# A start stage in hand-written order, and decode logits by one multiply-and-sum instruction of VectorE per 128 channels

## The chip, the cores and the metric

The kernel runs on one NeuronCore of a Trainium2 chip. The metric is the device time of one execution in microseconds (us), as the median of several runs. The engines are called PE (TensorE, matmuls), PEld (its weight load), DVE (VectorE), ACT (ScalarE), POOL (GpSimd) and SP (SyncE, which only issues transfers here).

## The reference

One inference step of a decoder layer with two parallel branches: stick-breaking attention and a gated short convolution. 512 prompt rows with 16 learned rows ahead of them, and 8 decode sequences of 4 rows with 512 cached positions each, in pages of 128.

```python
h = rmsnorm(x, g_pre)                                        # (560 rows, 2048)
q, k, v, ga, cb, cc, ch, gc, ma, mc = jnp.split(h @ w_in, split_offsets(), axis=-1)
a = stick_breaking(q, k, v, ...) * silu(ga)                  # 8 heads of 128 channels
c = cb * conv3_causal(cc * ch) * silu(gc)
m = sigmoid(ma + b_ga) * (a @ w_pa) + sigmoid(mc + b_gc) * (c @ w_pc)
y = x + rmsnorm(m @ w_out, g_post)

def stick_breaking(q, k, v, q_pos, k_pos, b_sb):
    z = einsum('bqhd,bkhd->bhqk', q, k) * HEAD_DIM ** -0.5 + b_sb
    mask = k_pos < q_pos
    log_keep = where(mask, log_sigmoid(-z), 0.0)
    after = cumsum(log_keep, axis=3, reverse=True) - log_keep
    attn = where(mask, exp(log_sigmoid(z) + after), 0.0)
    return einsum('bhqk,bkhd->bqhd', attn, v)
```

For the decode rows the keys and values of the past are read from the paged cache through `page_table`. All arrays are fp32.

## The kernel before

**Split products.** Each fp32 operand of a large product is held as a rounded part ("hi", fp32r) and the remainder ("lo"). A product is three matmuls: hi x hi, hi x lo, lo x hi. ACT makes the hi part of a weight block by a cast (`whi`, 128x1024, L236, L309 in the start), DVE the lo part by a subtraction (`wlo`, L237, L290 in the start). A weight block is 8 tiles of 128x128; PE does 24 matmuls with it for one range of tokens. Three hi and three lo blocks are buffered (`whl`), five raw ones (`wraw`), which SP's queue loads.

**The start.** The 560 token rows come in five blocks, 0 to 4 (`XT`; block 4 has the last 8 prompt rows, the 32 decode rows and 8 learned rows). `norm_stats` loads a block and takes its sum of squares on ACT (L195); `rstd_of` takes the root by a logarithm and an exponential on ACT (L129, L130) and five Newton instructions on DVE (L133 to L137). `norm_half` scales half of the channels on DVE (`hn`, L205), transposes them on PE in two groups of four into PSUM tiles (L213), and copies those into `h_hi` on ACT (L219) and `h_lo` on DVE (L224). The queries of four heads (`FIRST`) are projected meanwhile (L297), head by head: blocks 0 and 1 first with the hi weights alone, and when blocks 4, 2 and 3 are there the missing terms and the other tokens.

**The heads.** For four heads (`head_now`) k, v and q are projected and attention is done at once; for the other four (`head_later`) k and v are projected and kept. `natural` transposes k or v into row order through a PSUM tile into `nat` (one buffer), from which POOL's queue writes the outputs.

**The decode logits.** `decode_steps` is a generator; each step handles one page for half of the heads of one decode sequence: 4 heads, 4 rows, 128 cached positions on the partitions. DVE multiplies the page with the queries of two rows at a time (`pr`, 128x1024, L689, twice), and the sums over 128 channels are taken on ACT by eight or twelve copies that accumulate (`junk`, L695) and on DVE by a reduction of the rest (L698). 6 of 16 units of 4 pages (24 steps) run among the heads ("part"), 40 among the gate projections ("logits"). `dec_step` and `dec_group` say where: `dec_group` is called after each pair of column blocks of the gate and convolution projections, 32 times up to the last logits.

**The gates.** Each pair of 128-column blocks is done by `seven`, seven block products (L887) with sums of weight blocks (`s`) on DVE (L899, L902, L910, L915).

**What sets the order.** The program is written in one order, and a scheduler reorders it by its own costs, except instructions wrapped in `pin` (`tc.keep_in_program_order`), which keep their written order among one another on their engine. Every engine runs its queue in order.

## Time and profile before

| | us |
|---|---|
| median of 3 runs (lowest, highest) | 1638.24 (1635.78, 1639.5) |
| the profiled execution | 1638.43 |
| its span | 1636.8 |
| PE busy | 1596.0 (98%) |
| PEld busy | 1534.2 (94%) |
| DVE busy | 1259.1 (77%) |
| ACT busy | 969.5 (59%) |
| POOL busy | 232.2 (14%) |

The shares are means over stages. The start lasts to about 86 us of the span, the heads to 397, the gate and convolution projections to about 1163, the two branch products to about 1444, and the last product and normalization to the end. Matmuls are pipelined and their ends are modelled, so the count of matmuls in a stretch says more on PE than its busy time. A wait is put down to the engine that came last by the profile.

### The profile page before, as it was taken

To read this page: it belongs to the slowest core of one execution; us is meant where nothing else is said; L and a number is where in the kernel's file an instruction comes from. 1 tells how busy PE (TensorE), PEld (TensorE's weight loads), DVE (VectorE), ACT (ScalarE), POOL (GpSimd) and SP (SyncE) were. 2 spreads that over 40 slices of the span, in tenths; PEclk is the share of its full clock that TensorE was granted. 3 is DMA by queue.
4 is the path that set the end of the run, shared out by engine and by line. 5 is a ranking of instruction groups with operands and counts; after the bars stand their busy time and mean duration, and the time that the engine had idled before them with its cause. 6 is when DMAs were issued, how large, how long until landed. Compare 5 with 4: busy or idle time off the path is not lost.

```text
span 1636.8 us, 31603 instructions
## 1 busy us (share of the span) xinstructions
PE 1596.0 (98%) x12172; PEld 1534.2 (94%) x12172; DVE 1259.1 (77%) x1730; ACT 969.5 (59%) x2528; POOL 232.2 (14%) x418
## 2 busy tenths in 40 slices
PE   7999999999999999999999999999999999999997
PEld 6999999999999999999999999989877799999997
DVE  4537887797988988888988888876565567887776
ACT  6237887755775656565676667686544453355562
POOL 0033233322101000100011011002122110000000
PEclk7999999999999999999999999999999999999999
DMA  9254554545554444343555554446888545533345
GB/s 228 77 171 143 157 163 138 152 121 171 157 155 136 130 130 130 116 141 114 148 150 151 156 175 147 128 130 202 263 265 246 179 141 165 183 89 101 106 124 192
DMA packets 306813, 252.72 MB, mean 154 GB/s; under 512 B 11522, under 2 KB 276806, under 8 KB 305846
## 3 DMA queue, kind: packets, MB, share of 16 engines
q1 hardware_dynamic: 278165, 160.45, 34.3%
q0 software_dynamic: 28368, 89.98, 16.9%
q8 instruction: 95, 1.56, 0.4%
q14 instruction: 57, 0.46, 0.1%
q10 hardware_dynamic: 128, 0.27, 0.1%
HBM read 217.95 MB, written 32.71 MB: 153 GB/s over the span
## 4 chain that ended last, share of the span: by engine, by line
PE 75%; ACT 6%; DMA 5%; DVE 4%; issue 3%; POOL 0%; DVEq 0%; SPq 0%; POOLq 0%; ACTq 0%
PE mm L887 24%; PE mm L252 24%; PE o L887 20%; ACT junk L695 3%; PE tp L784 2%; ACT whi L236 2%; PE z L614 1%; DMA raw<-in_w_in 1%; PE o L624 1%; DVE pr L689 1%; DMA gt<-gate_scr 1%; DVE wlo L237 1%; PE z L545 1%; PE z L1319 1%; DMA kpage<-in_cache_k 1%
## 5 line engine op out<-in xcount | busy, mean ns | idle before, releaser
L236 ACT CAST whi<-raw 128x1024 fp32r<-128x1024 f32 x247 | 258.9, 1049 | 253.6 <-PE o L887 75.6
L237 DVE TENSOR_TENSOR wlo<-raw,whi 128x1024 fp32r<-128x1024 f32 x247 | 301.5, 1221 | 56.7 <-ACT whi L236 45.4
L887 PE MATMUL mm<-h_hi,whi 128*128 128x272 f32 (+1 forms) x1152 | 333.8, 290 | 2.8 <-ACT whi L236 2.8
L887 PE MATMUL mm<-h_lo,whi 128*128 128x272 f32 (+1 forms) x1152 | 332.4, 289 | 0.0
L887 PE MATMUL mm<-h_hi,wlo 128*128 128x272 f32 (+1 forms) x1152 | 331.6, 290 | 0.0
L887 PE MATMUL o<-t_hi,whi 128*128 128x272 f32 (+1 forms) x864 | 253.1, 293 | 8.7 <-ACT o L901 5.0
L887 PE MATMUL o<-t_hi,wlo 128*128 128x272 f32 (+1 forms) x864 | 250.8, 290 | 1.3 <-DVE wlo L237 1.3
L887 PE MATMUL o<-t_lo,whi 128*128 128x272 f32 (+1 forms) x864 | 250.6, 290 | 0.0
L237 DVE TENSOR_TENSOR wlo<-s,whi 128x1024 fp32r<-128x1024 f32 x126 | 154.2, 1224 | 100.5 <-ACT whi L236 100.2
L887 PEld LDWEIGHTS mm<-h_hi,whi 128*128 128x128 f32 x1152 | 217.7, 189 | 5.4 <-ACT whi L236 3.7
L887 PEld LDWEIGHTS mm<-h_hi,wlo 128*128 128x128 f32 x1152 | 216.6, 189 | 0.6 <-DVE dr L412 0.4
L887 PEld LDWEIGHTS mm<-h_lo,whi 128*128 128x128 f32 x1152 | 217.1, 188 | 0.1
L695 ACT ACTIVATE junk<-pr 128x128 f32<-128x128 f32 x592 | 182.6, 309 | 28.5 <-DVE pr L689 16.3
L236 ACT CAST whi<-s 128x1024 fp32r<-128x1024 f32 x126 | 131.5, 1044 | 96.9 <-PE o L887 30.8
L252 PE MATMUL mm<-h_hi,whi 128*128 128x280 f32 (+1 forms) x640 | 188.1, 294 | 0.0
L252 PE MATMUL mm<-h_hi,wlo 128*128 128x280 f32 (+1 forms) x640 | 188.0, 295 | 0.0
L252 PE MATMUL mm<-h_lo,whi 128*128 128x280 f32 (+1 forms) x640 | 187.6, 293 | 0.0
L887 PEld LDWEIGHTS o<-t_hi,whi 128*128 128x128 f32 x864 | 163.6, 189 | 15.5 <-ACT o L901 6.1
L887 PEld LDWEIGHTS o<-t_hi,wlo 128*128 128x128 f32 x864 | 163.8, 190 | 2.2 <-DVE wlo L237 2.2
L887 PEld LDWEIGHTS o<-t_lo,whi 128*128 128x128 f32 x864 | 164.4, 190 | 0.0
L689 DVE TENSOR_TENSOR pr<-kpage,qb 128x1024 f32<-128x1024 f32 x128 | 152.3, 1218 | 10.7 <-DMA qb<-q_scr 6.5
L252 PEld LDWEIGHTS mm<-h_hi,whi 128*128 128x128 f32 x640 | 121.4, 190 | 0.7
(392 smaller groups left out, 3402.3 us busy)
## 6 DMA issues: line engine op xcount, KB each, us to landing
raw<-in_w_in SPq DMA_DIRECT2D x192, 512.0 KB, 4.3
kpage<-in_cache_k POOLq DMA_DIRECT2D x64, 256.0 KB, 3.4
qb<-q_scr POOLq DMA_DIRECT2D x32, 512.0 KB, 5.7
vpage<-in_cache_v POOLq DMA_DIRECT2D x64, 256.0 KB, 6.1
raw<-in_w_out SPq DMA_DIRECT2D x32, 512.0 KB, 4.0
gate_scr<-g POOLq DMA_DIRECT2D x32, 272.0 KB, 3.5
gt<-gate_scr POOLq DMA_DIRECT2D x16, 544.0 KB, 4.2
raw<-in_w_pc SPq DMA_DIRECT2D x16, 512.0 KB, 5.9
```

Source lines behind the costliest of these rows:

```text
L236: act.copy(hi, x)
L237: dve.tensor_sub(lo, x, hi.bitcast(F32))
L252: pe.matmul(o, lhsT=w, rhs=r[:, t0:t1], start=(k == 0 and n == 0), stop=(k == nk - 1 and n == 2))
L545: pe.matmul(zt[:m, c0:c0 + n], lhsT=l[:, s0:s0 + m], rhs=r[:, ts:ts + n], start=(c0 == 0 and i == 0), stop=(i == 2), skip_group_check=True)
L614: pe.matmul(o, lhsT=l, rhs=x, start=False, stop=(i == len(ops) - 1), skip_group_check=True)
L624: pe.matmul(ot[:, ts - NMETA:ts - NMETA + n], lhsT=l[:m, st, :], rhs=x[:m, c0:c0 + n], start=False, stop=(g == GROUPS[-1] and i == 2), ski ...
L689: dve.tensor_mul(pr, kt.unsqueeze(1).broadcast_to([P, 2, 512]), qt))
L695: act.activation(junk, pr[:, t, h * P:(h + 1) * P], AF.Copy, accum_out=z_all[:, pg, b, 4 * hf + h, 2 * i + t:2 * i + t + 1])
L784: pe.matmul(po[32 * j:32 * (j + 1), :], lhsT=lhs, rhs=rhs, start=(pg == 0), stop=(pg == NPG), tile_position=(0, 32 * j), skip_group_check= ...
L887: pe.matmul(o, lhsT=l[:, k, :], rhs=r, start=(start and k == 0 and m == 0), stop=(stop and k == 7 and m == 2), skip_group_check=True)
L1319: pin(pe.matmul(o, lhsT=(m1, m2)[h][:, k + 8 * (q == 1), ts], rhs=two[h][q == 2][:, :, k, :], start=(n == 0), stop=(n == 47)))
```

## The change

Three parts, in words and then in the diff.

1. **The start** is written out by hand and pinned on every engine, SP's queue too. A block's load is a step of its own (`x_load`) apart from its statistics. The weights of the four early heads come in eight chunks, each with 256 input channels of all four heads (`q_load`), rather than in eight blocks of one head each; the raw bytes are the same. `q_chunk` does all three terms of a chunk for the 256 tokens of blocks 0 and 1, into four accumulators in two PSUM banks; the other 296 tokens follow for all chunks, head by head. Two of the four copies of the norm's weight move from DVE to ACT, the Newton steps of blocks 2 and 4 from DVE to POOL, and the transposes go round five PSUM tiles instead of four.
2. **The logits.** The two multiplies, the accumulating copies on ACT and the reduction on DVE become 16 DVE instructions a page, each of which multiplies 128 channels of a head with a row's query and sums them. In the built program each is two entries of DVE's queue: the instruction, and a read of its sum.
3. **Buffers and places.** `nat` has two buffers and `qn` four instead of one. Head 0's first decode step moves from behind its k to behind its attention; the first gate groups make 0, 2, 2, 2 steps instead of 2, 1, 2, 1, and the later ones 1, 2 by turns so that all 40 are done by group 32. Some POOL transfers near the two places are pinned.

```diff
-    def rstd_of(eng, out, ss, tmp, n, w=1, later=False):
+    def rstd_of(eng, out, ss, tmp, n, w=1, later=False, fix=lambda ins: ins):
...
-        act.activation(r, ss, AF.Ln, bias=eps_c[:n], scale=1.0 / D)
-        act.activation(r, r, AF.Exp, scale=-0.5)
+        fix(act.activation(r, ss, AF.Ln, bias=eps_c[:n], scale=1.0 / D))
+        fix(act.activation(r, r, AF.Exp, scale=-0.5))
...
-        with tc.high_priority():
-            act.activation(sq, xt, AF.Square, accum_out=ss)
-            newton = rstd_of(dve, rs, ss, tmp, n, later=True)
-        return (i, n, xt, rs), newton
+        pin(act.activation(sq, xt, AF.Square, accum_out=ss))
+        return (i, n, xt, rs), rstd_of(eng, rs, ss, tmp, n, later=True, fix=pin)
...
+    def q_load():
+        c = len(q_raw)
+        raw = wraw.tile([P, 8, P], F32, tag="raw", name="raw")
+        pin(nc.sync.dma_start(raw.rearrange("p (k h) c -> p k (h c)", k=2),
+                              win[2 * c * P:2 * (c + 1) * P, GATE_Q:GATE_Q + FIRST * P].rearrange(
+                                  "(k p) c -> p k c", p=P)))
+        q_raw.append(raw)
...
+    def q_product(o, h, k, n, start, stop):
+        t0, t1 = START[n]
+        hi, lo = (by_k(x[k // 2])[:, k % 2, h, :] for x in (q_hi, q_lo))
+        for m, (l, r) in enumerate(((hi, h_hi), (hi, h_lo), (lo, h_hi))):
+            pin(pe.matmul(o, lhsT=l, rhs=r[:, k, t0:t1], start=(start and m == 0), stop=(stop and m == 2),
+                          skip_group_check=True))
...
+    X[0], X[1] = x_load(0), x_load(1)
+    for _ in range(3):
+        q_load()
+    X[2] = x_load(2)
+    X[0], newton0 = norm_stats(X[0])
+    g_copy(0), g_copy(1)
+    g_copy(2), g_copy(3)
+    X[1], newton1 = norm_stats(X[1])
+    newton0(pin)
+    h00, l00 = norm_half(0, X[0])
+    h01, l01 = norm_half(1, X[0])
+    h00()
+    newton1(pin)
+    q_high()
+    h10, l10 = norm_half(0, X[1])
+    h01()
+    l00()
+    h11, l11 = norm_half(1, X[1])
...
+    l10()
+    q_high()
+    q_low()
+    h11()
+    q_chunk(0)
+    l01()
...
-        qn = hp.tile([TS, P], F32, name="qn", bufs=1)
+        qn = hp.tile([TS, P], F32, name="qn", bufs=4)
...
-        kn = hp.tile([P, 5, P], F32, name="nat", bufs=1)
+        kn = hp.tile([P, 5, P], F32, name="nat", bufs=2)
...
-                            pr = d1.tile([P, 2, 512], F32, name="pr", bufs=2)
-                            tc.keep_in_program_order(
-                                dve.tensor_mul(pr, kt.unsqueeze(1).broadcast_to([P, 2, 512]), qt))
-                            n = 2 if i == 0 else int(said == "logits" and pg % 2)
-                            if n:
-                                for t in range(n):
-                                    for h in range(4):
-                                        junk = d1.tile([P, P], F32, name="junk", bufs=1)
-                                        act.activation(junk, pr[:, t, h * P:(h + 1) * P], AF.Copy,
-                                                       accum_out=z_all[:, pg, b, 4 * hf + h, 2 * i + t:2 * i + t + 1])
-                            if n < 2:
-                                dve.reduce_sum(
-                                    z_all[:, pg, b, 4 * hf:4 * hf + 4, 2 + n:4].rearrange("p h t -> p t h"),
-                                    pr[:, n:].rearrange("p t (h d) -> p t h d", d=P), axis=mybir.AxisListType.X)
+                            for t in range(2):
+                                for h in range(4):
+                                    junk = d1.tile([P, P], F32, name="junk", bufs=2)
+                                    dve.tensor_tensor_reduce(
+                                        out=junk, in0=kt[:, h * P:(h + 1) * P], in1=qt[:, t, h * P:(h + 1) * P],
+                                        scale=1.0, scalar=0.0, op0=ALU.mult, op1=ALU.add,
+                                        accum_out=z_all[:, pg, b, 4 * hf + h, 2 * i + t:2 * i + t + 1])
...
-        if n <= 31:
-            dec_step(1 if 4 < n <= 20 else 1 + n % 2, "logits")
-        elif n == 32:
-            dec_step(64, "logits")
-            dec_step(1)
+        if n <= 32:
+            dec_step((0, 2, 2, 2)[n - 1] if n <= 4 else 1 if n <= 20 else 1 + n % 2, "logits")
```

**ACT's queue in the start, before** (`xt_161` is token block 1, `sq`/`ss` its squares and their sum, `rtmp` the root, `raw`/`whi` weight blocks):

```order
L195 ACTIVATE sq_164,ss_163<-xt_161 128x2048
L309 CAST whi_172<-raw_170 128x1024
L129 ACTIVATE rtmp_166<-ss_163,eps_c_78 128x1
L309 CAST whi_176<-raw_174 128x1024
L130 ACTIVATE rtmp_166<-rtmp_166 128x1
```

**The same place now** (`xt_154` is block 1):

```order
L200 ACTIVATE sq_178,ss_177<-xt_154 128x2048
L130 ACTIVATE rtmp_180<-ss_177,eps_c_78 128x1
L131 ACTIVATE rtmp_180<-rtmp_180 128x1
L224 CAST h_hi_87<-z_191 128x4x128
L224 CAST h_hi_87<-z_196 128x4x128
L310 CAST whi_220<-raw_156 128x1024
```

The two activations of the root stand right behind the squares, and the first weight cast behind block 0's first copies.

**DVE's queue in the start now**, from block 1's first scaled half to the second weight low (`z`, `tp`, `o` are the PSUM tiles of the transposes; `z_203` holds block 0's third group):

```order
L209 SCALAR_TENSOR_TENSOR hn_222<-xt_154,rs_179,g_bc_92 128x1024
L228 TENSOR_TENSOR h_lo_88<-z_191,h_hi_87 128x4x128
L228 TENSOR_TENSOR h_lo_88<-z_196,h_hi_87 128x4x128
L209 SCALAR_TENSOR_TENSOR hn_238<-xt_154,rs_179,g_bc_92 128x1024
L228 TENSOR_TENSOR h_lo_88<-o_224,h_hi_87 128x4x128
L228 TENSOR_TENSOR h_lo_88<-z_229,h_hi_87 128x4x128
L315 TENSOR_TENSOR wlo_266<-raw_156,whi_220 128x1024
L228 TENSOR_TENSOR h_lo_88<-z_203,h_hi_87 128x4x128
L228 TENSOR_TENSOR h_lo_88<-tp_208,h_hi_87 128x4x128
L315 TENSOR_TENSOR wlo_296<-raw_158,whi_264 128x1024
```

Weight lows stand among the token copies, and the copy out of `z_203`, whose PSUM buffer the last transposes of block 1 take over, stands behind the first weight low; before, all four copies of block 0 came ahead of block 1's second half, and no weight low stood here.

**DVE's queue in a convolution group, before** (one decode step among the block sums and weight lows):

```order
L902 TENSOR_TENSOR s_8404<-s_8404,raw_8396 128x1024
L1007 TENSOR_TENSOR cv_7864<-o_8147,cv_7864 128x272
L689 TENSOR_TENSOR pr_8365<-kpage_8363,qb_8109 128x1024
L689 TENSOR_TENSOR pr_8383<-kpage_8363,qb_8111 128x1024
L237 TENSOR_TENSOR wlo_8468<-s_8404,whi_8467 128x1024
L698 TENSOR_REDUCE z_all_894<-pr_8383 128x4
L237 TENSOR_TENSOR wlo_8498<-raw_8402,whi_8497 128x1024
```

**and now**, a part of one step:

```order
L972 TENSOR_TENSOR c_6755<-mm_6572,s2_6691 128x274
L754 ISA junk_6534,z_all_892<-kpage_6517,qb_6470 128x128
L754 ISA z_all_892 128x1
L754 ISA junk_6536,z_all_892<-kpage_6517,qb_6470 128x128
L754 ISA z_all_892 128x1
L241 TENSOR_TENSOR wlo_6874<-s_6840,whi_6873 128x1024
L754 ISA junk_6538,z_all_892<-kpage_6517,qb_6470 128x128
L754 ISA z_all_892 128x1
L754 ISA junk_6540,z_all_892<-kpage_6517,qb_6470 128x128
L754 ISA z_all_892 128x1
L956 TENSOR_TENSOR s_6840<-s_6840,raw_6832 128x1024
```

The pairs of a step lie in ones and twos, in places in longer runs, between the sums and weight lows.

More of the change, by code (lines that the diff above doesn't have):

```diff
@@ L345, in hybrid_step_kernel @@
[L345 to L356 removed]
+    q_high()
+    q_chunk(1)
+    X[2], newton2 = norm_stats(X[2], pool)
+    q_low()
+    for _ in range(2):
+        q_load()
+    q_chunk(2)
+    X[4], newton4 = norm_stats(X[4], pool)
+    newton2()
+    h20, l20 = norm_half(0, X[2])
+    q_high()
@@ L518, in v_proj @@
             act.copy(vr[:, s], ob)
[L519 removed]
+        vn = hp.tile([P, 5, P], F32, name="nat", bufs=2)
         vs = hp.tile([TS, P], F32, name="ks", bufs=1)
```

199 lines of the change are left out of this document (107 added, 92 removed).

## The prediction

> **What bounds the kernel now.** I read the page's busy lines first, then the busy time by stretches, then the timeline of the start, then the waits of the few stretches where TensorE (PE) is short of work. First the page's span and PE line, then four stretches (columns: PE, PEld, VectorE (DVE), ScalarE (ACT), GpSimd (POOL) busy, granted clock, DMA share, GB/s).
>
> ```profile
> span 1636.8 us, 31603 instructions
> PE 1596.0 (98%) x12172; PEld 1534.2 (94%) x12172; DVE 1259.1 (77%) x1730; ACT 969.5 (59%) x2528; POOL 232.2 (14%) x418
> ...
> 0.00:26.07 26.07, 14.49 (x66) 11.97 (x66) 12.71 (x31) 15.63 (x24) 2.17 (x9) 0.67 1.02 247
> 26.07:85.60 59.53, 57.44 (x442) 56.45 (x443) 30.70 (x53) 19.36 (x37) 2.20 (x4) 0.97 0.39 106
> 128.00:397.00 269.00, 269.00 (x2065) 262.99 (x2065) 224.76 (x309) 195.75 (x625) 81.34 (x144) 1.00 0.47 142
> 397.00:1088.00 691.00, 678.78 (x5329) 674.52 (x5328) 595.55 (x661) 450.06 (x1251) 65.06 (x115) 1.00 0.49 145
> ```
> The sum is made against this execution, 1638.4 us with its 1636.8 us span; that is 0.2 us from the median of the runs, 1638.24. PE is busy 98% of it, so removing work from DVE or ACT pays only where PE waits for it. PE lacks most in the first 26.07 us, at a granted clock of 0.67. From 128 to 397 us (the heads) and from 397 to 1088 us (gate projections with decode logits) PE has work nearly throughout, and DVE is second: 224.76 of 269 us (84%) and 595.55 of 691 us (86%). The slack that new DVE work can use is 44 and 95 us.
>
> **The start.** The timeline of before, on the way to the first product:
>
> ```profile
> 10.52 1.91 ACT L195 ACTIVATE sq<-xt 128x2048 f32<-128x2048 f32 x1 [2.08 <-DMA xt<-in_x_prompt]
> 12.43 1.03 ACT L309 CAST whi<-raw 128x1024 fp32r<-128x1024 f32 x1
> ...
> 15.90 1.04 ACT L309 CAST whi<-raw 128x1024 fp32r<-128x1024 f32 x1 [2.25 <-DMA raw<-in_w_in]
> ...
> 17.09 0.16 DVE L134 TENSOR_TENSOR rtmp<-rtmp 128x1 f32<-128x1 f32 x1 [3.98 <-ACT rtmp L130]
> ...
> 17.86 1.28 DVE L205 SCALAR_TENSOR_TENSOR hn<-xt,rs,g_bc 128x1024 f32<-128x1024 f32 x1
> ...
> 21.02 1.29 DVE L224 TENSOR_TENSOR h_lo<-z,h_hi 128x512 fp32r<-128x512 f32 x2 [1.88 <-ACT h_hi L219]
> ...
> 21.76 1.97 PE L213 MATMUL z<-ident,hn 128*128 128x128 f32 x8 [6.64 <-DVE h_lo L224]
> ...
> 26.07 1.01 PE L297 MATMUL mm<-h_hi,whi 128*128 128x256 f32 x3 [2.34 <-ACT h_hi L219]
> ...
> 28.80 0.42 PE L297 MATMUL mm<-h_hi,whi 128*128 128x256 f32 x1
> ...
> 29.02 0.38 PE L297 MATMUL mm<-h_lo,whi 128*128 128x256 f32 x1
> ...
> 29.35 0.28 PE L297 MATMUL mm<-h_lo,whi 128*128 128x256 f32 x1
> ...
> 29.47 0.28 PE L297 MATMUL mm<-h_hi,whi 128*128 128x256 f32 x1
> ```
> and the last product of the four early heads:
>
> ```profile
> 85.30 0.30 PE L297 MATMUL mm<-h_hi,wlo 128*128 128x296 f32 x1
> ```
> The second token block's Square ends at 12.4 us, but ACT's order puts two weight casts between it and the two activations of its root; the second waits for a weight load until 15.90. The Newton steps on DVE therefore wait 3.98 us and the scaled tile hn starts at 17.86. PE idles to 21.76, and the first product runs at 26.07.
>
> The change writes that order by hand. The casts stand behind the root, so it is through at about 13.1 (Square's end and some 0.7 us, an estimate, for the accumulator read and two one-element activations), and the five Newton steps end at 13.9 (17.09 to 17.86 is 0.77 us for four of them). For the rest of the walk:
>
> ```profile
> L205 DVE SCALAR_TENSOR_TENSOR hn<-xt,rs,g_bc 128x1024 f32<-128x1024 f32 x8 | 10.2, 1281 | 0.2
> ...
> L290 DVE TENSOR_TENSOR wlo<-raw,whi 128x1024 fp32r<-128x1024 f32 x8 | 9.7, 1221 | 12.6 <-PE z L297 12.6
> ```
> hn of the block's first half runs 13.9 to 15.2, two h_lo to 16.4 (0.65 each from the 1.29 us pair at 21.02), hn of the second half to 17.6, two h_lo to 18.8, the first weight low to 19.9, and then the h_lo that frees the PSUM tile of the block's last four transposes: 20.6. Those transposes take 0.9 us at the half clock (1.97 for 8 at 21.76), so the first product starts at about 21.5, not 26.07: 4.6 us sooner. All 26.07 us before it moved 247 GB/s; at that rate the 8.8 MB of tokens and four heads' weights (the same bytes before and now, in longer runs) are in by 38 us, and the last token block's Square stands behind the eighth weight cast on ACT, which by the same walk ends at about 44, so the loads are covered. SP's queue: tokens 0 and 1, three weight chunks, block 2, block 4, five more chunks, block 3; block 3 is the late one, with 6 us to spare.
>
> Behind the first product the matmuls are the same (384 products), but they come chunk by chunk with all three terms. Before, 26.07 to 85.6 is 59.5 us with 2.1 idle; eight transposes of it (1.7 us at the half clock) now stand ahead: 55.7 remain. Products start at the slow clock in both: 0.22 us apart at 28.80, 0.12 at 29.35, some 3 us of them. New waits that I find by laying the two queues side by side: block 4's second hn stands behind the fifth weight low on DVE, and PE lacks it for about 1.2 us; block 3's copies stand behind two result copies on ACT, about 0.8 us. So the stage ends at 21.5 + 55.7 + 2.0 = 79.2, against 85.6. I take **-6.5 us**, and -10 (no new waits, a warmer clock) to 0 (a load or the GpSimd root late) as ends. What becomes the limit there is DVE and ACT, not the loads.
>
> **Two buffers for the natural-order copy.** The wait, and the stretches around it:
>
> ```profile
> PE tp L445 <- ACT nat L443: 2.2, 1, 2.2
> ```
>
> ```profile
> 113.00:118.00 5.00, 5.00 (x42) 4.96 (x42) 2.65 (x4) 2.58 (x10) 1.67 (x3) 1.00 0.94 264
> 118.00:123.00 5.00, 3.83 (x31) 3.61 (x29) 2.29 (x3) 1.93 (x10) 0.67 (x2) 1.00 0.93 312
> 123.00:128.00 5.00, 3.95 (x21) 3.94 (x22) 3.18 (x7) 3.27 (x6) 2.29 (x4) 0.68 0.44 137
> ```
> PE makes 42 matmuls in an undisturbed 5 us, 31 and 21 in the next two: a stop of 2.2 us behind an output transfer and then a granted clock of 0.68. The missing 11 and 21 matmuls at 0.12 us are 3.8 us, less for the longer 32-bit ones among them. With two copies (and four for qn) the transfer need not have left. I take **-3.5**; ends -4 and 0 (the first page's wait, one decode step earlier or later, takes its place).
>
> **First page of the second decode part.** The waits from 380 to 430 us and the instruction behind them:
>
> ```profile
> PE o L887 <- ACT o L901: 1.4, 1, 1.4
> ```
>
> ```profile
> 406.24 2.36 DVE L689 TENSOR_TENSOR pr<-kpage,qb 128x1024 f32<-128x1024 f32 x2 [3.06 <-DMA kpage<-in_cache_k]
> ```
> DVE stood 3.06 us for a page just requested; PE lost 1.4 us. The change takes the step out of the first gate group (0, 2, 2, 2 steps, where it was 2, 1, 2, 1), so the page has a group's time to land: **-1.4**, ends -1.4 and 0. The number of steps stays 24 and 40. The pinned GpSimd transfers cost nothing: GpSimd is busy 65 of 691 us.
>
> **The logits.** What a page costs now (group rows, then DVE and ACT timelines):
>
> ```profile
> L689 DVE TENSOR_TENSOR pr<-kpage,qb 128x1024 f32<-128x1024 f32 x128 | 152.3, 1218 | 10.7 <-DMA qb<-q_scr 6.5 <-DMA kpage<-in_cache_k 3.1 <-ACT junk L695 0.9
> L698 DVE TENSOR_REDUCE z_all<-pr 128x8 f32<-128x1024 f32 x44 | 53.4, 1214 | 0.3
> ...
> L698 DVE TENSOR_REDUCE z_all<-pr 128x4 f32<-128x512 f32 x20 | 13.6, 682 | 0.0
> ```
>
> ```profile
> 483.03 2.35 DVE L689 TENSOR_TENSOR pr<-kpage,qb 128x1024 f32<-128x1024 f32 x2
> 485.30 1.22 DVE L910 TENSOR_TENSOR raw<-raw 128x1024 f32<-128x1024 f32 x1
> ...
> 506.02 0.16 DVE L970 TENSOR_TENSOR u<-c,cv 128x2 f32<-128x2 f32 x1
> 506.10 0.40 DVE L971 TENSOR_TENSOR u<-c,cv 128x240 f32<-128x240 f32 x1
> 506.42 0.18 DVE L972 TENSOR_TENSOR u<-c,cv 128x32 f32<-128x32 f32 x1
> 506.52 1.22 DVE L237 TENSOR_TENSOR wlo<-raw,whi 128x1024 fp32r<-128x1024 f32 x1
> ```
>
> ```profile
> 487.26 0.31 ACT L695 ACTIVATE junk<-pr 128x128 f32<-128x128 f32 x1
> 487.48 0.18 ACT L695 ACTIVATION_READ_ACCUMULATOR junk<-pr 128x1 f32 x1
> 487.57 0.40 ACT L959 COPY cv<-c 128x274 f32<-128x274 f32 x1
> ```
> Back to back, a 1024-element DVE instruction takes 1.135 us (two from 483.03 to 485.30). A heads step is three of them, 3.4 us; a gates step has the full or the half reduction by turns, 2.27 + (1.13 + 0.60)/2 = 3.13 us. Now a step is 16 pairs on DVE: a multiply-and-sum over 128 channels and a read of its sum. Nothing shows that pair. From below: 240 elements start to start take 0.32 us and 32 take 0.10, so 128 take about 0.20, and the read, if free, nothing: 0.20, 3.2 us a step. From above: the ACT pair shows 0.22 from main to read (a full drain, not an overlap); on DVE, main and read each drained are 0.28 + 0.16 (from 0.18 for 32, 0.40 for 240 and 0.16 for 2 elements) = 0.44, 7.0 us a step. I take 0.20 + 0.08 (2 elements, start to start) = 0.28, since these DVE rows do overlap, and ACT's read lets the next one start after 0.09: 4.5 us a step.
>
> DVE's load then grows by 24 x 1.1 = 26 us in the heads and 40 x 1.35 = 54 in the gates: 251 of 269 and 650 of 691 (93, 94%). Both fit; ACT loses 592 pairs of 0.31 us, 183 us, so its casts are ready sooner. But pairs now stand in runs ahead of weight lows for which PE waits, and a page's buffer is held through 16 pairs rather than two multiplies, with GpSimd's next page request waiting for it (three buffers at one step per 21.5 us: covered). With 6% of slack I allow **+4 us** of new PE waits, ends -5 (ACT's relief wins) and +15.
>
> The page "Vector Engine (DVE) Microarchitecture Reference" of the Trainium skill (Points that are easy to get wrong) speaks against the change: it says that a scalar-tensor-tensor instruction with two SBUF sources wider than bf16 halves its throughput, as no port is left for the accumulator. The row above has two such sources without a sum, at 1281 ns against 1221 for the plain subtraction, and is not halved; with a sum no run here shows it. By that rule the pair would be about 0.41 us, an estimate from that page, and the sum the second rival's.
>
> **Sum.** -6.5 - 3.5 - 1.4 + 4 = -7.4: 1638.4 - 7.4 = **1631**.
>
> **Rivals.** (1) The pairs are cheap or ACT's relief counts: DVE waits add nothing, all terms at their better end: -10 - 4 - 1.4 - 5, 1618. For it: ACT is freed in every group. Against: DVE is fuller than ACT in both stages. (2) DVE becomes the bound, and the kernel is slower. Capacity ends at 3.4 + 44/24 = 5.24 us a step in the heads (a pair of 0.33) and 3.13 + 95/40 = 5.5 in the gates (0.345). Beyond both, each 0.01 us of a pair costs 64 x 16 x 0.01 = 10 us. The start's gains (11.4) are used up at about 0.35, a loss of 0.2% stands at 0.352, and at 0.41 the time is 1638.4 - 11.4 + 24 x 3.16 - 44 + 40 x 3.43 - 95 = 1701. For it: ACT's drained read; against: overlapping DVE rows. (3) DVE fits on average but not in conv groups and two-step groups, whose waits eat the gain: +11, 1638. (4) The start's gain does not come, since a load or the root on GpSimd is late: 1638.4 - 1 = 1637.5.
>
> **How the numbers follow.** A change under 0.2% (3.3 us) can't be told from none here. Forecast 0.48, rival 1 0.12, rival 2 0.22, rivals 3 and 4 0.18. Faster: forecast and rival 1, 0.60; same: rivals 3 and 4, 0.18; slower: rival 2, 0.22. The range goes from rival 1, 1618, up into rival 2 as far as a pair of 0.363 (1638.4 + 0.0143 x 1024 = 1653), which leaves out about 0.18. The forecast's own range is 1622 to 1636.
>
> **What would show it.** The first product near 21.5 and the last of the early heads near 79; no wait for nat near 118 us; the new DVE pair's start-to-start time against 0.28 and 0.345; DVE busy near 251 and 650 us in the two stretches (shifted by 10 us). The prediction is wrong if the pair is over 0.33, if PE waits for weight lows by more than 4 us in all, or if the early heads end after 83.

## The result, and the profile after

The changed kernel takes 1615.62 us (median of 4 runs, 1612.98 to 1616.69), against 1637.23 for the kernel before, run beside it: a ratio of 0.9859 with a 95% interval of 0.9841 to 0.9878. That is 21.6 us less by the medians and 23.1 by the ratio. Figures of single parts below, taken between kernels that were run at different times, can differ by up to 4 us in the same way. The forecast was 7.4 less; the time lies 2.4 us below the lower end of the range. The execution profiled took 1616.69 us.

The page of the changed kernel (span 1615.1 us), its busy line, then the group of the new instruction (busy us, mean ns of one | idle time before it):

```profile
PE 1595.0 (99%) x12172; PEld 1533.7 (95%) x12172; DVE 1268.6 (79%) x3574; ACT 754.0 (47%) x1339; POOL 238.0 (15%) x428
...
L754 DVE CUSTOM_DVE_ANT_0 junk<-kpage,qb 128x128 f32<-128x128 f32 x1024 | 246.3, 288 | 4.7 <-DMA qb<-q_scr 4.3
```

DVE's busy time has hardly moved (1259.1 us before), ACT's fell by 215 us. The stretches of the changed kernel, cut at the first product, the end of the early heads, the first gate product and the 33rd gate group:

```profile
0.00:22.57 22.57, 19.34 (x75) 16.23 (x75) 12.46 (x30) 12.94 (x20) 0.99 (x7) 1.00 0.89 248
22.57:78.30 55.73, 54.96 (x435) 54.51 (x434) 29.32 (x43) 23.16 (x42) 8.13 (x14) 1.00 0.39 125
78.30:369.30 291.00, 291.00 (x2239) 284.10 (x2238) 225.47 (x1013) 137.91 (x281) 91.61 (x164) 1.00 0.50 151
369.30:1051.40 682.10, 680.50 (x5392) 679.80 (x5391) 613.45 (x1828) 308.93 (x452) 69.68 (x121) 1.00 0.50 148
```

and the same two last stretches of the kernel before, cut at the same instructions:

```profile
85.40:380.70 295.30, 293.07 (x2239) 285.99 (x2238) 227.13 (x318) 204.49 (x665) 91.20 (x162) 0.99 0.49 148
380.70:1076.20 695.50, 686.41 (x5392) 682.33 (x5391) 600.55 (x660) 448.18 (x1244) 68.87 (x120) 1.00 0.49 144
```

The same 5392 matmuls of the gates take 682.1 us where they took 695.5, and PE is busy in all but 1.6 of them. The chain of the start, by the timeline after: `hn` of the second token block at 16.87, the first product at 22.57, the last of the early heads at 78.14.

```profile
16.87 1.29 DVE L209 SCALAR_TENSOR_TENSOR hn<-xt,rs,g_bc 128x1024 f32<-128x1024 f32 x1
...
22.57 0.56 PE L321 MATMUL mm<-h_hi,whi 128*128 128x256 f32 x1
...
78.14 0.30 PE L321 MATMUL mm<-h_hi,wlo 128*128 128x296 f32 x1
```

The largest of PE's waits after; the one for `nat` is gone, and what is left in the gates is 2.1 us, 1.6 of it for `c` and 0.5, below the lines shown, for a weight cast:

```profile
PE mm L256 <- DVE gt L1148: 3.3, 1, 3.3
PE o L216 <- DVE hn L209: 2.0, 2, 1.3
PE o L941 <- DVE c L967: 1.6, 2, 0.8
PE tp L158 <- DVE neg_one L112: 1.3, 1, 1.3
```

And how the pairs stand on DVE, here around one set of gate sums (c, L967) and weight lows (wlo, L241):

```profile
897.09 1.22 DVE L964 TENSOR_TENSOR raw<-raw 128x1024 f32<-128x1024 f32 x1
898.22 0.29 DVE L754 CUSTOM_DVE_ANT_0 junk<-kpage,qb 128x128 f32<-128x128 f32 x1
898.43 0.09 DVE L754 DVE_READ_ACCUMULATOR2_ANT z_all<- 128x1 f32 x1
898.43 0.29 DVE L754 CUSTOM_DVE_ANT_0 junk<-kpage,qb 128x128 f32<-128x128 f32 x1
898.64 0.09 DVE L754 DVE_READ_ACCUMULATOR2_ANT z_all<- 128x1 f32 x1
898.64 0.44 DVE L967 TENSOR_TENSOR c<-o,s 128x272 f32<-128x272 f32 x1
899.00 1.22 DVE L241 TENSOR_TENSOR wlo<-raw,whi 128x1024 fp32r<-128x1024 f32 x1
```

Two things are to be seen. A pair takes 0.21 us from start to start (898.22 to 898.43): the read of the sum starts together with the next instruction and costs nothing, so a step is 16 x 0.21 = 3.4 us. And the pairs do not stand in runs of 16. Counted in the order of DVE's trace there are 366 runs, 253 of exactly two pairs and 48 of one; the longest has 18. In the kernel before, the same place in the queue looked like this:

```profile
851.08 2.35 DVE L689 TENSOR_TENSOR pr<-kpage,qb 128x1024 f32<-128x1024 f32 x2
853.34 1.22 DVE L910 TENSOR_TENSOR raw<-raw 128x1024 f32<-128x1024 f32 x1
854.48 0.44 DVE L913 TENSOR_TENSOR c<-o,s 128x272 f32<-128x272 f32 x1
854.83 1.22 DVE L237 TENSOR_TENSOR wlo<-raw,whi 128x1024 fp32r<-128x1024 f32 x1
```

Here 2.35 us of multiplications stand ahead of the sum and the low part. PE's waits, then DVE's for weight blocks, in groups 21 to 32 of the kernel before:

```profile
PE o L887 <- DVE c L913: 2.8, 3, 1.9
PE mm L887 <- ACT whi L236: 2.2, 3, 0.7
```

```profile
DVE s L899 <- DMA raw<-in_w_in: 6.5, 7, 2.6
```

The longest wait for `c`, 1.9 us, is the one behind the instructions shown above, and for 3.3 us from 855.30 the granted clock is 0.50. DVE's waits for blocks belong to this too: SP's queue asks for a block when an old one is done with (in these groups it waits 242 us for DVE and 4 for ACT), so a long stretch on DVE can also make the next block late. In the changed kernel DVE has no such wait in these groups.

**All kernels by stage.** Read off PE's timeline of each: the first and the last early product; then the us that the heads take, gate groups 1 to 4, the 16 convolution groups, groups 21 to 32 (a group is 168 matmuls of `seven`), and from there to the first matmul of the last product ("rest"). Medians are of the runs compared; before stood at 1635.6 to 1637.9 beside them.

| kernel | first product, end | heads | 1-4 | 5-20 | 21-32 | rest | median |
|---|---|---|---|---|---|---|---|
| before | 26.1, 85.3 | 295.4 | 86.9 | 344.7 | 263.9 | 368.1 | 1637.2 |
| after | 22.6, 78.1 | 291.1 | 86.3 | 342.0 | 253.8 | 371.1 | 1615.6 |
| e1 logits only | 25.5, 84.7 | 295.7 | 86.5 | 340.9 | 253.8 | 364.4 | 1620.6 |
| e2 start only | 19.6, 75.2 | 297.1 | 96.0 | 347.0 | 263.2 | 370.0 | 1643.1 |
| e5 start undone | 25.4, 83.9 | 291.5 | 85.9 | 341.9 | 253.8 | 371.1 | 1623.4 |
| e6 logits undone | 22.6, 78.0 | 292.1 | 88.2 | 345.7 | 263.7 | 370.9 | 1629.5 |
| e7 old step places | 19.6, 75.2 | 291.1 | 85.6 | 340.9 | 253.8 | 364.2 | 1606.9 |
| e3 copies of the page | 22.6, 78.1 | 296.9 | 86.6 | 354.0 | 260.2 | 372.2 | 1637.8 |
| e11 copies of an own tile | 19.1, 74.4 | 293.3 | 86.0 | 345.4 | 255.2 | 372.9 | 1622.0 |
| e8 21 pairs | 19.5, 75.5 | 291.2 | 91.6 | 341.3 | 253.9 | 372.3 | 1620.4 |
| e9 26 pairs | 22.6, 78.1 | 291.2 | 114.7 | 341.0 | 253.9 | 403.2 | 1670.7 |
| e4 multiply, reduce | 22.6, 78.0 | 318.7 | 95.3 | 433.0 | 253.6 | 369.4 | 1742.5 |
| e12 the same, spread | 22.6, 78.1 | 303.0 | 104.6 | 349.0 | 271.1 | 373.8 | 1671.4 |
| e13 pairs in runs | 19.6, 75.2 | 303.2 | 92.5 | 354.7 | 273.0 | 371.2 | 1660.8 |
| e14 pairs pinned | 19.2, 74.5 | 291.2 | 86.2 | 340.9 | 253.7 | 369.5 | 1611.9 |
| e10 values sooner | 19.1, 75.9 | 291.1 | 86.0 | 341.1 | 258.0 | 352.0 | 1598.2 |

From before to after: start -7.2, heads -4.3, groups 1 to 4 -0.6, convolution groups -2.7, groups 21 to 32 -10.1, rest +3.0.

### The profile page after: what moved, and what is told of

Its sections match the earlier page's. It is cut to its first block, busy times and chain, and to the rows that moved or that the text cites. A ratio compares the mean times of both kernels' runs of the same rounds, so it can differ in the third digit from the quotient of the medians.

```text
span 1615.1 us, 32344 instructions
## 1 busy us (share of the span) xinstructions
PE 1595.0 (99%) x12172; PEld 1533.7 (95%) x12172; DVE 1268.6 (79%) x3574; ACT 754.0 (47%) x1339; POOL 238.0 (15%) x428
## 4 chain that ended last, share of the span: by engine, by line
PE 95%; DMA 2%; DVE 2%; ACT 1%; issue 0%; DVEq 0%; POOL 0%; SPq 0%; ACTq 0%
PE mm L941 31%; PE mm L256 27%; PE o L941 23%; PE tp L841 3%; PE mm L321 2%; PE z L677 1%; PE o L687 1%; PE z L321 1%; PE z L608 1%; PE z L1373 1%; DMA sg<-a_scr 1%; PE tp L505 0%; DMA raw<-in_w_pc 0%; DMA qb<-q_scr 0%; PE z L1227 0%
## 5 line engine op out<-in xcount | busy, mean ns | idle before, releaser
L241 DVE TENSOR_TENSOR wlo<-raw,whi 128x1024 fp32r<-128x1024 f32 x247 | 301.8, 1223 | 87.8 <-ACT whi L240 86.5
L754 DVE CUSTOM_DVE_ANT_0 junk<-kpage,qb 128x128 f32<-128x128 f32 x1024 | 246.3, 288 | 4.7 <-DMA qb<-q_scr 4.3
L941 PEld LDWEIGHTS mm<-h_lo,whi 128*128 128x128 f32 x1152 | 216.8, 188 | 0.1
L241 DVE TENSOR_TENSOR wlo<-s,whi 128x1024 fp32r<-128x1024 f32 x126 | 154.4, 1225 | 63.6 <-ACT whi L240 62.4
L256 PEld LDWEIGHTS mm<-h_lo,whi 128*128 128x128 f32 x640 | 120.3, 188 | 0.8
```

What stands on the lines that cost most here:

```text
L241: dve.tensor_sub(lo, x, hi.bitcast(F32))
L256: pe.matmul(o, lhsT=w, rhs=r[:, t0:t1], start=(k == 0 and n == 0), stop=(k == nk - 1 and n == 2))
L754: dve.tensor_tensor_reduce(out=junk, in0=kt[:, h * P:(h + 1) * P], in1=qt[:, t, h * P:(h + 1) * P], scale=1.0, scalar=0.0, op0=ALU.mult, o ...
L941: pe.matmul(o, lhsT=l[:, k, :], rhs=r, start=(start and k == 0 and m == 0), stop=(stop and k == 7 and m == 2), skip_group_check=True)
```

## The parts apart: the logits or the start (e1, e2)

e1 is the kernel before with the edit of the logits alone:

```diff
-    pr = d1.tile([P, 2, 512], F32, name="pr", bufs=2)
-    tc.keep_in_program_order(dve.tensor_mul(pr, kt..., qt))
-    ...  # ACT copies that sum, DVE reduction
+    junk = d1.tile([P, P], F32, name="junk", bufs=2)
+    dve.tensor_tensor_reduce(out=junk, in0=kt[...], in1=qt[...], ..., accum_out=z_all[...])
```

> The kernel before with the logits edit alone (16 multiply-and-sum pairs a page; start, buffers and places of the steps as before). Theory A, relief of ACT: a pair costs DVE 0.21 us, so DVE carries the same load as before and ACT loses the 592 accumulating copies; the waits of TensorE among the gates go. The start and the nat copy stay as they were (7 and 4 us). Expected 1627, gate groups at 21.1 to 21.4 us, also the groups that took 26 and 27 us. Theory B, places and order: the gates gain from the moved steps and the new order, not from the instruction: 1635 to 1638, groups of 26 and 27 us stay.

Measured: 1620.64 us, ratio 0.9894 (0.9875 to 0.9913). The edit that the prediction charged with +4 us gives 17 by itself: 10.1 in groups 21 to 32, 3.8 in the convolution groups, 3.7 in the rest (the 33rd group takes 23.6 us where it took 27.5, with one wait of 3.1 us for a copy on ACT). The gate groups came as theory A said, most at 21.1 to 21.4 us, and the time is 6 us below its 1627.

e2 is the kernel before with the start (from `load_x` to the last early product) of the changed one, and nothing else.

> The kernel before with the start written out by hand alone (logits, buffers and places of the steps as before). Theory A: the early heads end near 78 us rather than 85, the rest is moved as a whole: 1630, -7. Theory B: the start's order also moves what follows it, and half of the gain of the gates comes with it: 1625 or less.

Measured: 1643.11 us, ratio 1.0033 (1.0020 to 1.0047): neither theory, but slower than before, though its early heads end 10 us sooner. It gives 9.1 back in the first four gate groups, all of it in the first. Its waits there, and the stretch:

```profile
DVE s L962 <- DMA raw<-in_w_in: 8.1, 1, 8.1
...
PE o L950 <- DVE c L976: 5.3, 1, 5.3
...
390.00:410.00 20.00, 14.74 (x102) 14.52 (x102) 14.12 (x16) 9.39 (x27) 2.05 (x4) 0.83 0.60 194
```

DVE stood 8.1 us for a weight block whose transfer was late, PE stood 5.3 for DVE, and the granted clock fell to 0.83.

## The parts taken away (e5, e6)

e5 is the changed kernel with the start of before.

> The changed kernel with the start of the kernel before (casts in the scheduler's order, term by term products); logits, buffers and step places as changed. Theory A (ScalarE's relief makes room, so the start's 7 us are kept where ScalarE is free): early heads end near 85, and the time is 1615.6 + 7 = 1622 to 1623. Theory B (the start's gain is given back in the first gate groups whatever ScalarE does, as it was with the start alone): the logits alone gave 1620.6, the buffers and places some 4 more, so 1615 to 1617, no slower than the whole change.

Measured: 1623.42, ratio 0.9923 (0.9909 to 0.9938): theory A. With the new logits the start is worth 7.8 us by the medians (10.5 by the ratios, 5.8 by the ends of the early heads in the two profiles), and it is not given back. The heads stay at 291.5, where e1, with the old single buffers, has 295.7: the 4 us of the heads belong to the buffers and the places of the heads' steps.

e6 is the changed kernel with the logits of before.

> The changed kernel with the logits of before (two VectorE multiplies, ScalarE's summing copies and a VectorE reduction a page); start, buffers and step places as changed. Theory A (the start's gain needs ScalarE free): ScalarE is at 50 to 57 of 86 us a gate stretch again, the first four gate groups take 90 us or more, and what is left are the buffers: 1634 to 1640. Theory B (the parts add up): 1615.6 + 17.3, the logits' own gain = 1633 or, with start -7.2 and buffers -4 and first page -1.4 kept, 1625 to 1633.

Measured: 1629.49, ratio 0.9958 (0.9945 to 0.9971): within the second range of theory B, by which the parts add up. Groups 21 to 32 are back at 263.7, but the first four groups take 88.2, not the 96.0 of e2. So theory A, that the start's gain needs ACT free, is refuted there. What e6 has and e2 has not are the buffers and the places, with no step in the first gate group; the first 18 us of its gates, where e2 had 15.68 of 17.70, are full:

```profile
370.00:388.00 18.00, 18.00 (x146) 17.96 (x145) 14.19 (x15) 11.06 (x16) 5.24 (x9) 1.00 0.48 141
```

Which of the two, buffers or places, keeps the weight block on time was not run apart.

## Is it ScalarE's relief? (e3, e11)

e3 puts 592 summing copies back on ACT, as many as before, of the page:

```diff
+    for x in range(na):            # 8 a page in the heads, 8 or 12 in the gates
+        act.activation(ja, kt[:, ...128 columns...], AF.Copy, accum_out=za[:, x:x + 1])
```

> The changed kernel with 592 more ACT copies that sum 128 channels of a page into a tile that nothing reads, eight or twelve a step as before the change; DVE's work is as in the changed kernel. Theory A: ACT is as full as before the change, so the waits for casts and for PSUM copies on ACT come back in the gates: +6 to +10 us, 1622 to 1626. Theory B: ACT is off TensorE's path, 1615 to 1617.

Measured: 1637.78, ratio 0.9996 (0.9981 to 1.0012), above both theories. All 22 us are gone, and taken alone this would read as proof that ACT's relief is the gain. ACT's waits in the gates say something else:

```profile
ACT ja L762 <- DMA kpage<-in_cache_k: 73.0, 35, 5.2
```

The copies wait at the head of ACT's queue for a page that has not landed, and the weight casts stand behind them. e11 takes that away: the same number of copies, of a tile that the page's last pair leaves.

```diff
+    last = i + t + h == 5
+    junk = d1.tile([P, P], F32, name="jl" if last else "junk", bufs=3 if last else 2)
     ...
+        act.activation(ja, junk, AF.Copy, accum_out=za[:, x:x + 1])
```

> The changed kernel with as many ScalarE summing copies as the kernel before makes (8 a page in the heads, 8 or 12 in the gates, 592), here of a tile that the page's last multiply-and-sum leaves and nothing else waits for, so that no page's buffer is held longer. Theory A (ScalarE's time is what counts: its casts of the weights come late again): as with the copies of the page, 1632 to 1642. Theory B (in that experiment the copies held the page's buffer and so delayed the next page and VectorE): 1616 to 1622.

Measured: 1621.97, ratio 0.9915 (0.9901 to 0.9928): theory B. In the gates, e11 and e3 load ACT alike:

```profile
367.70:1054.30 686.60, 682.41 (x5392) 680.13 (x5391) 612.20 (x1828) 448.44 (x1252) 69.59 (x121) 1.00 0.49 147
```

```profile
375.00:1075.80 700.80, 686.74 (x5392) 680.98 (x5391) 612.06 (x1828) 445.18 (x1252) 69.45 (x121) 1.00 0.48 144
```

448 and 445 us of ACT, but 686.6 against 700.8 us of span, the first being e11. Against the changed kernel e11 loses 6 us by the medians and 9 by the ratios. So ACT's occupancy alone is worth a third to a half of the 17, and of the 10.1 us in groups 21 to 32 only 1.4. Something else in the old logits cost the rest.

## Is it VectorE's load? (e4, e8, e9)

e4 does the logits on DVE alone by two multiplications and two reductions of 1024 elements a page.

> The changed kernel with two multiplies and two reductions over 1024 elements on DVE a page in place of the 16 pairs: 4.54 us of DVE a step, the load that the prediction gave to the pairs (4.5), and no ACT work. Theory A (a filled DVE costs TensorE little while ACT is free): DVE busy near 660 of 682 us in the gates, 1616 to 1619. Rival, the prediction's own term (some 4 us of waits beyond what was there before): 1625 to 1630. If DVE's order is the limit at 96 to 97% full: over 1630.

Measured: 1742.49, ratio 1.0642 (1.0620 to 1.0663). Of the three theories the last, over 1630, came, but no theory had a loss of this size. Without the pin the scheduler put 35 of its steps into 433 us, and DVE is busy without a gap there:

```profile
492.00:600.00 108.00, 91.18 (x606) 87.39 (x605) 108.00 (x120) 34.45 (x56) 13.85 (x24) 0.87 0.45 133
```

That shows what a full DVE does (PE 91 of 108 us), but not whether the load or its piling is to blame. e8 and e9 add 5 and 10 pairs a page to the changed kernel:

```diff
+    for x in range(5):             # e9: 10
+        dve.tensor_tensor_reduce(out=junk, in0=kt[...], in1=qts[1][...], ..., accum_out=zx[:, x:x + 1])
```

> The changed kernel with five more multiply-and-sum instructions a page into a tile that nothing reads: 21 of 0.21 us is 4.4 us a step, the load of VectorE that the prediction took (4.5); 64 x 5 x 0.21 = 67 us more on VectorE. Theory A (load of that size lies in VectorE's slack; only ScalarE's relief decided): heads and gate groups stay within 1 per cent, 1616 to 1620, and the prediction's price was wrong without consequence. Theory B (the price of the pair carried the miss: at 4.4 us a step VectorE's runs hold up weight lows): +4 to +25 us, 1620 to 1640.

Measured: 1620.43, ratio 0.9906 (0.9888 to 0.9925). This lies at the edge between the two theories. 67 us more on DVE cost 5 us by the medians (8 by the ratios). By stages nearly all of it is in the first gate group, which takes 26.9 us instead of 21.8, and none is where DVE is fullest:

```profile
458.30:799.60 341.30, 341.29 (x2698) 340.85 (x2697) 328.37 (x1058) 146.73 (x224) 29.27 (x51) 1.00 0.46 135
799.60:1053.50 253.90, 253.90 (x2018) 253.90 (x2017) 242.93 (x894) 121.17 (x168) 28.02 (x49) 1.00 0.52 159
```

> The changed kernel with ten more multiply-and-sum instructions a page into a tile that nothing reads: 26 of 0.21 us, 5.5 us a step, which the prediction's count of VectorE's room gave as the point where it is full (5.24 in the heads, 5.5 in the gates). With 21 a page VectorE was already 328 of 341 us busy in the conv groups and 243 of 254 behind them. Theory A (VectorE becomes the bound where its room ends): the 42 us more in the gates find about 25 us of room (5 in the heads' end, 11 in groups 20 to 32, the rest in the last groups), so 20 to 35 us more than with 21: 1640 to 1655. Theory B (what doesn't fit slides behind the gates at no cost, since only the values wait for it): 1620 to 1628.

Measured: 1670.66, ratio 1.0207 (1.019 to 1.0225): theory A in kind, but more than its 1655, and in other places. Heads and groups 5 to 32 are untouched; DVE's overflow comes out where the stages meet, in the first gate group and behind the gates:

```profile
PE mm L947 <- ACT whi L240: 25.9, 2, 25.3
PE mm L256 <- DVE gt L1154: 15.5, 4, 8.5
```

The first wait names ACT, but ACT's cast waits there for a sum on DVE: from 370 to 400 us DVE is busy for 29.86 of 30 us, mostly with the sums of token blocks that the gates need, and PE for 3.98.

## Is it the length of what stands in VectorE's queue? (e12, e13, e14)

e12 has the multiplications of e4 pinned, so that the steps spread over the groups as before; its load is that of e8.

```diff
+    pin(dve.tensor_mul(pr, kt.unsqueeze(1).broadcast_to([P, 2, 512]), qt))
+    dve.reduce_sum(z_all[...], pr..., axis=mybir.AxisListType.X)
```

> The changed kernel with two multiplications and two reductions of 1024 elements a page on VectorE (4 x 1.135 = 4.54 us a step, nothing on ScalarE), the multiplications kept in program order so that the steps spread over the groups as in the kernel before (in the earlier kernel of this kind they came 35 in 433 us). VectorE's load is that of 21 pairs a page (4.41 us, 1620), in instructions of 1.2 and 2.3 us and not of 0.2. Theory C (length: a long instruction stands ahead of the weight lows for which TensorE waits, a short one fits into VectorE's gaps): 1630 to 1650. Theory A (only ScalarE's relief and VectorE's total load count; the earlier loss was the piling): 1616 to 1624.

Measured: 1671.36, ratio 1.0206 (1.019 to 1.0222): theory C, and more of it. 4.54 us a step in instructions of 1.2 us cost 51 us more than 4.41 us a step in instructions of 0.21 (e8).

e13 keeps the changed kernel's very instructions, pins them in written order and gives the unread product 16 buffers; e14 pins them and keeps two.

```diff
-    junk = d1.tile([P, P], F32, name="junk", bufs=2)
-    dve.tensor_tensor_reduce(...)
+    junk = d1.tile([P, P], F32, name="junk", bufs=16)      # e14: 2
+    pin(dve.tensor_tensor_reduce(...))
```

> The changed kernel with all 16 pairs of a page pinned in program order and 16 buffers for their unread products, so that they come mostly in runs of 8 to 18 (3.4 us) and not one or two at a time; the same instructions, and as many a stretch as before. Theory C (length of what stands ahead): conv groups and groups 20 to 32 lose some 8 to 15 us against the same kernel with short runs: 1624 to 1632. Theory A: within 3 us of it, 1614 to 1619.

> The control of the one before: the 16 pairs pinned in program order in the same way, with the change's two buffers, so that they come mostly one or two at a time. Both theories: as the changed kernel, 1614 to 1618; anything above that is the price of the pinning itself.

Measured: e14 1611.93, ratio 0.9852 (0.9835 to 0.9868); e13 1660.82, ratio 1.0144 (1.0125 to 1.0163). The control is 2 us below its range; e13 is theory C in kind, 29 us above its range. 49 us lie between them, and the buffers of an unread tile are the only difference in the programs. In the order of DVE's trace e14 has 344 runs, most of two; e13 has 63, 20 of them of 16, and among the heads, which take 12 of the 49 us, up to 64 in a row. DVE's timeline of e13, from the first to the last of one run and what stands behind it:

```profile
863.36 0.28 DVE L754 CUSTOM_DVE_ANT_0 junk<-kpage,qb 128x128 f32<-128x128 f32 x1
...
866.55 0.28 DVE L754 CUSTOM_DVE_ANT_0 junk<-kpage,qb 128x128 f32<-128x128 f32 x1
866.76 0.08 DVE L754 DVE_READ_ACCUMULATOR2_ANT z_all<- 128x1 f32 x1
866.76 1.22 DVE L964 TENSOR_TENSOR raw<-raw 128x1024 f32<-128x1024 f32 x1
867.90 0.43 DVE L967 TENSOR_TENSOR c<-o,s 128x272 f32<-128x272 f32 x1
868.25 1.21 DVE L241 TENSOR_TENSOR wlo<-raw,whi 128x1024 fp32r<-128x1024 f32 x1
```

and PE's waits in the whole of it:

```profile
PE mm L941 <- DVE wlo L241: 15.8, 8, 2.9
PE mm L941 <- ACT whi L240: 6.5, 9, 0.8
PE mm L256 <- DVE wlo L241: 6.0, 3, 4.2
PE o L941 <- DVE wlo L241: 5.9, 4, 1.5
```

27.7 us of waits for `wlo` on DVE, where the changed kernel's list above, down to 1.3 us, has none. 3.4 us of pairs now stand ahead of the sum and the low part at once. DVE waits for late weight blocks again, 3.3 us in groups 21 to 32, where e14 has none. Of groups 21 to 32, where two steps and one alternate, every second takes 23.4 to 26.0 us in e13 and the others 21.1 to 21.5; in e14 all take 21.1 or 21.2; in the kernel before every second took 21.6 to 25.9, in the same alternation. Those are the 10 us of groups 21 to 32. e13 holds ACT's load at the new level, so a long stretch on DVE is enough to bring this pattern back.

That the second buffer paces the pairs (the third must wait for the first one's product, and the scheduler puts a weight instruction between) is read from the built order of e13 and e14. No run changed the scheduler itself.

## A faster version: the places of the steps (e7, e10)

e7 is the changed kernel with `dec_group` of before.

```diff
-    if n <= 32:
-        dec_step((0, 2, 2, 2)[n - 1] if n <= 4 else 1 if n <= 20 else 1 + n % 2, "logits")
+    if n <= 31:
+        dec_step(1 if 4 < n <= 20 else 1 + n % 2, "logits")
+    elif n == 32:
+        dec_step(64, "logits")
+        dec_step(1)
```

> The changed kernel with the gate groups' decode steps placed as before (2, 1, 2, 1 in the first four, the remaining logits and the first values in group 32). In the changed kernel the stretch from group 32 to the end is 371.1 us, in the kernel with the logits' edit alone, which keeps the old places, 364.4. Theory A (the later places push value matmuls behind the gates and cost that): the tail is 364 to 365, less 1.4 us lost for the first page: 1610 to 1612. Theory B (the tail's 6.7 us came of the old start or buffers, not of the places): 1616 to 1618.

Measured: 1606.9, ratio 0.9829 (0.9816 to 0.9842): theory A and some 3 us more. The places cost 8.7 us by the medians and 4.9 by the ratios; by stages, without the start, the difference is 8.7, of which 6.9 in the rest. In the changed kernel the generator's mark at the end of the logits uses up a call of its own, so softmax and values come two groups later. e10 goes the other way and takes two steps in groups 21 to 29:

```diff
+    if n <= 29:
+        dec_step(1 + n % 2 if n <= 4 else 1 if n <= 20 else 2, "logits")
+    elif n == 30:
+        dec_step(64, "logits")
+        dec_step(1)
```

> The kernel with the old step places (1606.9) with two steps in each of groups 21 to 29, so that the logits end and the decode's softmax begins in group 30 instead of 32 and the value matmuls start two groups (some 45 us) sooner. Theory A (a value matmul beside gate matmuls costs PE less, 0.19 us against 0.33 in the later projection): 30 or more of them move, 4 to 5 us: 1602 to 1604. Theory B (the tail's gain came from the wait for gt and the slow clock behind it alone, or VectorE's 6.8 us a group of pairs comes into PE's way): 1606 to 1612.

Measured: 1598.17, ratio 0.9762 (0.9748 to 0.9776), better than both theories and the best of all: 37 us less than the kernel before, run beside it, by the medians, and 39 by the ratio. What values cost: the busy time of PE on the 128 value matmuls, after (in the c projection; none stand ahead of it), then e7 (ahead of it and in it), then e10 (one record lies on the cut and is counted twice):

```profile
1140.20:1325.80 185.60, 42.40 (x128) 0.99 0.72 227
```

```profile
1046.70:1145.70 99.00, 6.13 (x32) 1.00 0.64 199
1145.70:1311.40 165.70, 31.07 (x96) 1.00 0.68 216
```

```profile
1046.00:1120.00 74.00, 8.67 (x40) 1.00 0.59 188
1120.00:1290.00 170.00, 16.69 (x89) 1.00 0.73 231
```

42.4, 37.2 and 25.4 us for the same work. The timelines, after and e10, show the difference:

```profile
1173.97 1.04 PE L841 MATMUL tp<-vpage,z_all 128*32 128x512 f32 x2
```

```profile
1066.10 1.06 PE L841 MATMUL tp<-vpage,z_all 128*32 128x512 f32 x6
```

Two value matmuls in a row take as long as six. Each writes one of four strips of 32 partitions, and neighbours overlap. In the changed kernel 30 of 38 such bursts are of two, in e7 23 of 33, in e10 only 6 of 21. This is read from the traces; no run changed the bursts alone.

## Why the prediction was right or wrong

**The bound.** That PE sets the time and DVE is second was right: PE is 99% busy after, and e9 shows DVE taking over.

**The start, -6.5.** Right by the number in the profiled execution: -7.2, the end at 78.1 against 79.2. That is in part luck, since one step came 3.0 us later than the walk had it, and two terms of it, 1.8 and 2.0 us, did not come. The first product came at 22.57, not 21.5. The scaled half `hn` that the walk had at 13.9 came at 16.87, since ACT takes the squares of block 1 only behind two of the four copies of the norm's weight, and these waited for slow matmuls. Behind it the walk lets the last transposes of block 1 wait for the first weight low and the copy out of `z_203` (1.8 us), and the text on DVE's queue ahead of the prediction says the same of that copy's buffer; but the transposes start at 21.80 and that copy at 22.79. And from the first to the last product it is 55.6 us, without the 2.0 of new waits. The walk also left out that the start has two forms: seven other profiles of the same start show the first product at 19.1 to 19.6 and an end of 74.4 to 75.9, the -10 of its better end. The difference stands in the 24 matmuls that spread g, after and then e14:

```profile
5.90 5.38 PE L176 MATMUL mm<-g_hl,pick 16*128 16x128 f32 x24
```

```profile
5.36 2.93 PE L176 MATMUL mm<-g_hl,pick 16*128 16x128 f32 x24
```

They ran at about half speed in one of them, and everything behind shifts by 3 us. The traces' records of the granted clock split in the same way: the first one at full speed begins at 4.4 to 6.4 us in the seven profiles of the better form, and at 17.3 to 24.4 in the other six, after among them (24.39). There the products start 0.21 us apart up to 24.2 us and 0.12 apart from 24.41. The clock of 1.00 that the view above gives for the first 22.57 us only means that no record falls into that time. So the 3 us go with the clock in the execution that was profiled. The Trainium skill ("TensorE: Matmul & The Clock Gate", Part 1, on the clock gate) says that the gate's window runs freely, so that the warm-up differs from run to run. The two rows fit that; no run here shows what sets the time of the first grant. Rival 4, that the start's gain doesn't come, holds for the start alone (e2), by a road that the prediction did not have: the weight block late at the first gate group, not a load or the root in the start.

**The buffers, -3.5.** Right: the wait for `nat` is gone, and the heads take 4.3 us less, in e5 too, which has the old start.

**First page of the second part, -1.4, and "the number of steps stays".** The groups 1 to 4 gained 0.6, and e7, with the old places, has them in 85.6 against 86.3: with the new logits the moved places gained nothing there. And the sentence on the number of steps looked at the logits only and not at what follows them: the places that save a page's wait put the values two groups later, and that costs 5 to 9 us (e7). The largest loss in the change was not in the sum at all.

**The logits, +4.** This is the step that failed: alone they are -17. Its three parts, one by one:
- The pair's price, 0.28 us, was too high: 0.21, the lower bound plus 0.01. Between 0.20 and 0.44 I chose by an addition for the read, which is free. The row is 0.21 us. The rule of the Trainium skill ("Vector Engine (DVE) Microarchitecture Reference", Points that are easy to get wrong), by which it would have been 0.41, is not borne out. But the price does not explain the miss: e8 gives DVE the 4.4 us a step that the forecast assumed, and still runs at 1620, 15 us less than the kernel before.
- "Pairs now stand in runs ahead of weight lows for which PE waits": this sentence made the sign. Most runs are of one or two pairs (301 of 366), and only three, among the heads, are longer than 13. Had they stood in runs, the change would have been a loss: e13, 1660.8.
- What the old logits cost was never in the sum. I asked what the new instructions would hold up, and not what the old ones already did: 2.35 us of multiplications ahead of sums and low parts, 10 us over groups 21 to 32. ACT's relief, allowed at 5 us, is 6 to 9 (e11).

None of the three signs that the prediction named for being wrong came: each of them looks for a change that does worse than forecast, and none for one that does better.

**The rivals.** Rival 1 forecast 1618, close to what came, with the pairs cheap as it said; of its reasons ACT's relief is a third to a half. Rival 2 put the point where DVE is full at 5.24 to 5.5 us a step. At 5.5 (e9) the kernel is already 35 us slower than the one before, run beside it, so the room was overstated: what PE needs from DVE at the seams between stages is not spread evenly. Rival 3's mechanism, DVE fitting on average and failing in two-step groups, is real, but in the old kernel and in e13.

**The sum by measured parts.** Logits -17.3 (e1), start -7.8 (e5), heads -4.3, places +8.7 (e7): -20.7, against -21.6 measured. By the ratios start and places are -10.5 and +4.9 and the sum is -27, against -23.1: the parts add up to within some 4 us, and the closer match by the medians is in part luck.

## What to carry to other kernels

On an engine that works in order and feeds the bound, look at the longest stretch that stands ahead of a critical instruction, not only at the busy share: 21 short instructions a page, mostly by twos, cost 5 to 8 us at a load at which four long ones cost 51 us more. How many buffers an unread output has can decide how a scheduler spreads the instructions that write it (e13 and e14). And before charging a change with what the new work will delay, price what the old work delays already; the waits of the same stretch, group by group, show it.

## What the hardware showed that was not expected

On DVE the accumulator's read (0.08 to 0.09 us) runs together with the next instruction, so a fused multiply-and-sum of 128 fp32 channels costs 0.21 us from start to start; ACT's summing copy of 128 elements takes 0.31 (L695 before). Value matmuls that write four strips of partitions by turns take 1.04 us for two in a row and 1.06 for six.
